# A large tile for the high parts of a pair, and wide blocks for the attention projection

## The chip, the cores and the metric
The kernel runs on one core of a Trainium2 chip. The metric is the time of one execution on the device, in microseconds (us). Before the change it is 1595.82 us, the median of three runs (1594.87 to 1597.53).

## The reference
One decoder layer over 256 tokens of width 2048, all in float32. `u` is the normed input. One projection `u @ w_in` gives q, k, v, z, xBC, dt and two gates. Attention and a state space mixer run side by side, each is projected to the model width, and the two are merged by gates:

```
out_a = attn @ w_attn_br[i]                      # (256 x 1024) @ (1024 x 2048)
out_s = y @ w_ssd_br[i]                          # (256 x 2048) @ (2048 x 2048)
merged = sigmoid(g_a) * out_a + sigmoid(g_s) * out_s
h = h + merged @ w_o[i]
h = h + (silu(f @ w_gate[i]) * (f @ w_up[i])) @ w_down[i]     # hidden width 5632
h = h + sigmoid(rmsnorm(h, g_ple[i]) @ w_ple_gate[i]) * (p[i] @ w_ple_proj[i])
```

## The kernel before
**Three products for one.** Every large product is made of float32 values split in a high part (a cast to the type fp32r) and a low part (value minus high part). A product is high x high, high x low and low x high, three matmuls of 128 x 128 by 128 x 512. The weights are read from memory in raw tiles `wr` of two rows of 128 and 512 columns (512 KB, pool of 4). ScalarE casts one into `wh` (pool of 4), VectorE subtracts into `wl` (pool of 3), and PE multiplies.

**Two kinds of blocks.** `nblock` (L178) makes one block of 512 output columns for both halves of the tokens. Each raw tile feeds 12 matmuls. `wide_block` (L281) makes two column blocks at once and goes over pairs `kp` of rows of 128. A plain pair takes two raw tiles and 24 matmuls. A pair listed in `forms` is done as a 2 x 2 x 2 product in seven block products instead of eight, 21 matmuls. For it VectorE makes four sums of the weights, `tr` (L329), which need both raw tiles; the sums are split into `th` (ScalarE, L337) and `tl` (VectorE, L338). Of the raw tiles, three quarters are also used as they are: both rows of the first one (`b11`, `b21`) and the second row of the second (`b22`), here called the plain blocks of the pair. They too are split on L337 and L338. PE takes first the products with the plain blocks (nine matmuls), then those with the four sums. The other factor of the seven products, the token forms, is prepared earlier (`token_forms`, L268). After the last such pair of a block four of the seven sums are combined into `mid` (L353 to L356), and after the block's end `settle` (L359) or `add_settled` (L364) joins them with the plain sums.

The pair's plain blocks use the pools of all plain tiles: two tiles of `wh` and two of `wl`, of which the second is only half used. `tr`, `th`, `tl`, `mid` and all activations come from the pool `big` of 17 tiles.

**The order of the work.** The attention projection is four `nblock`s over `attnT` (L985 to L989), each followed by two multiplications with the gate. Side work (transposes, the mixer, token forms) is queued in `side` and `heads` and taken from the queues by `pump` after each raw tile. A scheduler orders the program and gives each pool tile its place; an instruction waits for the last reader of the tile that had the place before. Each engine takes its instructions strictly in the order of its own queue.

The stages that matter: four `nblock`s for the first gate (L967), the attention projection (454 to 499 us), then wide blocks only: the second gate, the mixer's projection, `w_o`, eleven hidden blocks of gate and up, and three times two down blocks (to 1465 us). 40 pairs are done in seven products.

Of the kernel before, what the change touches and what calls it, by code (L numbers as in the profile page):

```python
# [15 lines left out]
ALU = mybir.AluOpType  # L16
# [45 lines left out]
def block_kernel(ctx: ExitStack, tc: tile.TileContext, x, x_t, p_t, positions, vecs, rows, g_final,  # L62
# [14 lines left out]
    def big(shape, dtype=F32, name="big"):  # L77
        return big_p.tile(shape, dtype, name=name, tag="big")
# [24 lines left out]
    def drain(*queues):  # L103
        for q in queues or (side,):
            while q:
                q.popleft()()
# [52 lines left out]
    def stat(tiles, k):  # L159
        return tiles[k // 4][:, 0, k % 4, :], tiles[k // 4][:, 1, k % 4, :]  # L160
# [10 lines left out]
    def rsqrt_mean(parts, out_r):  # L171

        n = out_r.shape[1]
        s = stat_p.tile([P, NT], F32, name="rms_s")[:, :n]
        nc.vector.tensor_reduce(out=s, in_=parts, op=ALU.add, axis=AX.X)
        nc.gpsimd.tensor_tensor(out=out_r, in0=s, in1=mhalf[:, :n], op=ALU.pow)
# [83 lines left out]
    def joined(tiles, kp):  # L260

        ks = slice(2 * (kp % 2), 2 * (kp % 2) + 2)
        sc = roll("fsc").rearrange("p (j t) -> p j t", j=2)
        src = tiles[kp // 2].bitcast(F32)
        nc.vector.tensor_tensor(out=sc, in0=src[:, 0, ks], in1=src[:, 1, ks], op=ALU.add)
        return sc
# [14 lines left out]
    def wide_block(halves, lhs, nk, forms, pumps=1):  # L281
# [19 lines left out]
        for kp in range(np_):  # L301
# [23 lines left out]
            for o, x, y in ((tr[:, 0], raw[0][:, 0], raw[1][:, 0]),  # L325
# [2 lines left out]
                            (tr[:, 3], tr[:, 2], raw[0][:, 1])):  # L328
                nc.vector.tensor_tensor(out=o, in0=x, in1=y, op=ALU.add)  # L329
            split = []  # L330
            for x, xh, xl in (
                    (raw[0], whi_p.tile([P, 2, NB], F32R, name="wh", tag="wh"),
                     wlo_p.tile([P, 2, NB], F32R, name="wl", tag="wl")),
                    (raw[1][:, 1:2], whi_p.tile([P, 2, NB], F32R, name="wh", tag="wh")[:, 1:2],
                     wlo_p.tile([P, 2, NB], F32R, name="wl", tag="wl")[:, 1:2]),
                    (tr, big([P, 4, NB], F32R, name="th"), big([P, 4, NB], F32R, name="tl"))):
                nc.scalar.copy(out=xh, in_=x)  # L337
                nc.vector.tensor_tensor(out=xl, in0=x, in1=xh.bitcast(F32), op=ALU.subtract)  # L338
                split.extend((xh[:, i], xl[:, i]) for i in range(x.shape[1]))
# [29 lines left out]
    def form_tiles(pairs, name):  # L369
        tile = big([P, 2, 4, 2, P], F32R, name=name)  # L370
        return {kp: tile[:, i] for i, kp in enumerate(pairs)}

    def column_pair(w, col0, jj):
        return tuple((w, col0 + (2 * jj + q) * NB) for q in range(2))
# [333 lines left out]
    def queue_xs(g, src):  # L708
# [69 lines left out]
        def flip(i):  # L778
            def run():
                xd = mix[g, "xd"]  # L780
                kp = 2 * g + i
                if kp == YPAIRS[0]:
                    yforms.update(form_tiles(YPAIRS, "yforms"))
                transpose_pair([xd[:, t, 1] for t in range(NT)], i * 2 * P, yT[g], 2 * i,
                               [vcol(V_GSSD, 4 * g + 2 * i + j) for j in range(2)],
                               yforms.get(kp))
            return run
# [176 lines left out]
    def cols(j):  # L964
        return slice(j * NB, (j + 1) * NB)

    for j in range(4):  # L967
        accs = nblock(w_in, GAO + j * NB, lhs_u, KD)
        for t in range(NT):
            nc.scalar.activation(out=merged[t][:, cols(j)], in_=accs[0][t], func=AF.Sigmoid,  # L970
                                 scale=r1[:, t:t + 1])
    drain(heads)
    UPAIRS = (3, 6)
    uforms = {}

    def u_forms(kp):
        def run():
            if kp == UPAIRS[0]:
                uforms.update(form_tiles(UPAIRS, "uforms"))
            token_forms(joined(uT, kp), uforms[kp])  # L980
        return run

    side.extend(u_forms(kp) for kp in UPAIRS)
    r2 = const.tile([P, NT], F32, name="r2")
    for j in range(4):  # L985
        accs = nblock(w_attn_br, j * NB, lambda k: stat(attnT, k), 8)
        for t in range(NT):
            nc.vector.tensor_tensor(out=merged[t][:, cols(j)], in0=accs[0][t],
                                    in1=merged[t][:, cols(j)], op=ALU.mult)  # L989

    drain()
    rsqrt_mean(ssq2, r2)
    mergedT = []

    def queue_flip(src, dst, j, gbase=None, forms={}):
# [17 lines left out]
        gates.append(parts)  # L1013
    mforms = form_tiles((5,), "mforms")
    for jj in range(2):
        sums, parts = wide_block(column_pair(w_ssd_br, 0, jj), lambda k: stat(yT, k), KD, yforms)
        for i in range(4):
            t, c = i // 2, cols(2 * jj + i % 2)
            settle(i, sums, parts)
            nc.vector.scalar_tensor_tensor(out=parts[i], in0=parts[i], scalar=r2[:, t:t + 1],  # L1020
                                           in1=gates[jj][i], op0=ALU.mult, op1=ALU.mult)
            nc.vector.tensor_tensor(out=merged[t][:, c], in0=merged[t][:, c], in1=parts[i],
                                    op=ALU.add)
        for q in range(2):
            queue_flip(merged, mergedT, 2 * jj + q, None, mforms)
# [239 lines left out]
```

## Time and profile before

| what | us |
|---|---|
| median of three runs | 1595.82 |
| lowest, highest | 1594.87, 1597.53 |
| the profiled execution | 1594.49 |
| its span, first to last instruction | 1592.8 |
| PE busy | 1574.0 (99%) |
| VectorE (DVE) busy | 1201.3 (75%) |
| ScalarE (ACT) busy | 844.2 (53%) |
| GpSimd (POOL) busy | 132.1 (8%) |

PE is matmul, PEld its weight load. The granted clock of PE is 0.998 of full over the span. Matmuls overlap in their pipeline: one of 512 columns shows some 0.39 us from its start to its end, but the next starts after 0.227 us. So what a product costs, and what PE loses at a wait, is read from start to start. A number in brackets at the end of a row is the engine's idle time before the row and what ended it.

### The profile page before, as it was taken

To read this page: it belongs to the slowest core of one execution; us is meant where nothing else is said; L and a number is where in the kernel's file an instruction comes from. 1 tells how busy PE (TensorE), PEld (TensorE's weight loads), DVE (VectorE), ACT (ScalarE), POOL (GpSimd) and SP (SyncE) were. 2 spreads that over 40 slices of the span, in tenths; PEclk is the share of its full clock that TensorE was granted. 3 is DMA by queue.
4 is the path that set the end of the run, shared out by engine and by line. 5 is a ranking of instruction groups with operands and counts; after the bars stand their busy time and mean duration, and the time that the engine had idled before them with its cause. 6 is when DMAs were issued, how large, how long until landed. Compare 5 with 4: busy or idle time off the path is not lost.

```text
span 1592.8 us, 19985 instructions
## 1 busy us (share of the span) xinstructions
PE 1574.0 (99%) x7298; PEld 1300.5 (82%) x7298; DVE 1201.3 (75%) x1507; ACT 844.2 (53%) x1073; POOL 132.1 (8%) x136
## 2 busy tenths in 40 slices
PE   9999999999999999999999999999999999999997
PEld 7988888888888888788788888788888878888886
DVE  8776766666666768788888788887878788788874
ACT  6654665555644554445655554455545444556653
POOL 1014224143210000000000000000000000000000
PEclk9999999999999999999999999999999999999999
DMA  8666435555646666655566655566665566655672
GB/s 270 177 198 185 136 105 158 158 161 157 178 157 183 210 199 213 209 195 189 173 199 195 198 188 197 185 210 193 193 196 177 194 203 199 220 189 185 200 228 87
DMA packets 152562, 296.63 MB, mean 186 GB/s; under 512 B 9536, under 2 KB 9664, under 8 KB 152080
## 3 DMA queue, kind: packets, MB, share of 16 engines
q1 hardware_dynamic: 151168, 290.76, 58.3%
q0 software_dynamic: 576, 3.47, 0.7%
q8 instruction: 57, 0.93, 0.2%
q10 hardware_dynamic: 720, 1.14, 0.2%
q14 instruction: 41, 0.34, 0.1%
HBM read 293.23 MB, written 2.10 MB: 185 GB/s over the span
## 4 chain that ended last, share of the span: by engine, by line
PE 92%; DVE 2%; DMA 2%; ACT 2%; issue 1%; POOL 0%; POOLq 0%; DVEq 0%; SPq 0%; ACTq 0%
PE aux L249 29%; PE acc L249 27%; PE acc L204 9%; PE acc L206 9%; PE acc L205 9%; PE aux L150 1%; DMA wr<-in_w_in_dram 1%; PE aux L754 1%; DMA wr<-in_w_gate_dram 1%; ACT th L337 1%; PE acc L150 1%; DVE tl L338 1%; PE aux L935 1%; PE aux L693 0%; ACT sc L899 0%
## 5 line engine op out<-in xcount | busy, mean ns | idle before, releaser
L309 ACT CAST wh<-wr 128x1024 fp32r<-128x1024 f32 x280 | 293.6, 1053 | 269.4 <-PE acc L249 97.2
L311 DVE TENSOR_TENSOR wl<-wr,wh 128x1024 fp32r<-128x1024 f32 x280 | 337.3, 1221 | 88.2 <-issue 35.8
L195 DVE TENSOR_TENSOR wl<-wr,wh 128x1024 fp32r<-128x1024 f32 (+1 forms) x172 | 227.6, 1330 | 119.6 <-PE acc L205 87.4
L193 ACT CAST wh<-wr 128x1024 fp32r<-128x1024 f32 (+1 forms) x172 | 173.7, 1013 | 167.9 <-PE acc L206 125.6
L249 PE MATMUL aux<-wh,flipT 128*128 128x512 f32 x736 | 237.8, 392 | 0.0
L249 PE MATMUL acc<-wh,flipT 128*128 128x512 f32 x640 | 208.4, 393 | 0.0
L204 PE MATMUL acc<-wh,uT 128*128 128x512 f32 (+1 forms) x512 | 200.3, 391 | 0.7 <-ACT cb L481 0.7
L206 PE MATMUL acc<-wh,uT 128*128 128x512 f32 (+1 forms) x512 | 194.2, 379 | 0.0
L205 PE MATMUL acc<-wl,uT 128*128 128x512 f32 (+1 forms) x512 | 193.9, 379 | 0.0
L249 PEld LDWEIGHTS aux<-wh,flipT 128*128 128x128 f32 x736 | 138.1, 188 | 28.3
L249 PE MATMUL aux<-wl,flipT 128*128 128x512 f32 x368 | 143.8, 391 | 0.6 <-DVE wl L311 0.6
L337 ACT CAST wh<-wr 128x1024 fp32r<-128x1024 f32 x80 | 66.8, 837 | 140.2 <-PE aux L249 62.4
L249 PEld LDWEIGHTS acc<-wh,flipT 128*128 128x128 f32 x640 | 120.2, 188 | 24.6 <-ACT wh L337 0.2
L249 PE MATMUL acc<-wl,flipT 128*128 128x512 f32 x320 | 124.6, 389 | 0.0
L338 DVE TENSOR_TENSOR tl<-tr,th 128x2048 fp32r<-128x2048 f32 x40 | 91.7, 2292 | 26.2 <-ACT th L337 26.1
L204 PEld LDWEIGHTS acc<-wh,uT 128*128 128x128 f32 x512 | 96.3, 188 | 18.1 <-issue 1.4
L205 PEld LDWEIGHTS acc<-wl,uT 128*128 128x128 f32 x512 | 96.4, 188 | 17.6 <-issue 1.0
L206 PEld LDWEIGHTS acc<-wh,uT 128*128 128x128 f32 x512 | 96.2, 188 | 17.8
L337 ACT CAST th<-tr 128x2048 fp32r<-128x2048 f32 x40 | 76.5, 1911 | 51.7 <-DVE tr L329 51.7
L249 PE MATMUL aux<-wh,actT 128*128 128x512 f32 x292 | 95.3, 393 | 0.0
L249 PE MATMUL acc<-wh,actT 128*128 128x512 f32 x292 | 93.6, 390 | 0.0
L338 DVE TENSOR_TENSOR wl<-wr,wh 128x1024 fp32r<-128x1024 f32 x80 | 76.2, 954 | 7.8 <-PE aux L249 4.0
(476 smaller groups left out, 2741.4 us busy)
## 6 DMA issues: line engine op xcount, KB each, us to landing
wr<-in_w_in_dram SPq DMA_DIRECT2D x144, 512.0 KB, 3.7
wr<-in_w_gate_dram SPq DMA_DIRECT2D x88, 512.0 KB, 3.7
wr<-in_w_up_dram SPq DMA_DIRECT2D x88, 512.0 KB, 4.1
wr<-in_w_down_dram SPq DMA_DIRECT2D x88, 512.0 KB, 4.4
wr<-in_w_ssd_br_dram SPq DMA_DIRECT2D x32, 512.0 KB, 4.3
wr<-in_w_o_dram SPq DMA_DIRECT2D x32, 512.0 KB, 4.0
wr<-in_w_ple_gate_dram SPq DMA_DIRECT2D x32, 512.0 KB, 4.9
wr<-in_w_in_dram SPq DMA_DIRECT2D x32, 256.0 KB, 3.9
```

The source lines that it names most:

```text
L150: nc.tensor.transpose(out=ps[:, j, t * P:(t + 1) * P], in_=src[t][:, c:c + P], identity=ident)
L193: nc.scalar.copy(out=wh, in_=wr)
L195: nc.vector.tensor_tensor(out=wl, in0=wr, in1=wh.bitcast(F32), op=ALU.subtract)
L204: nc.tensor.matmul(o, hi[:, ts], wh[:, kk, cs], start=(k == 0), stop=False)
L205: nc.tensor.matmul(o, hi[:, ts], wl[:, kk, cs], start=False, stop=False)
L206: nc.tensor.matmul(o, lo[:, ts], wh[:, kk, cs], start=False, stop=(k == nk - 1))
L249: nc.tensor.matmul(self.tile, a, b, start=self.first, stop=self.left == 0)
L309: nc.scalar.copy(out=wh, in_=wr)
L311: nc.vector.tensor_tensor(out=wl, in0=wr, in1=wh.bitcast(F32), op=ALU.subtract)
L337: nc.scalar.copy(out=xh, in_=x)
L338: nc.vector.tensor_tensor(out=xl, in0=x, in1=xh.bitcast(F32), op=ALU.subtract)
L754: nc.tensor.matmul(ps[:, es], m[:, t, e, :], xd[:, t, 0, es], start=True, stop=True)
```

## The change
The change has two parts. First, in a pair of seven products the high parts of the plain blocks go to a tile `sh` of the pool `big`, which also holds the low part of `b22`. The pair now takes no tile of `wh`, one of `wl` and four instead of three of `big`. Second, the attention projection becomes two wide blocks, with the pair `APAIR` = 2 of four in seven products. Its token forms lie in the free half of the tile of `yforms`. They and the two forms of `uT` are queued before the first gate's blocks, which pump one time more every fourth raw tile, and both queues are drained before the attention projection.

```diff
             split = []
+
+            sh = big([P, 4, NB], F32R, name="sh")
             for x, xh, xl in (
-                    (raw[0], whi_p.tile([P, 2, NB], F32R, name="wh", tag="wh"),
-                     wlo_p.tile([P, 2, NB], F32R, name="wl", tag="wl")),
-                    (raw[1][:, 1:2], whi_p.tile([P, 2, NB], F32R, name="wh", tag="wh")[:, 1:2],
-                     wlo_p.tile([P, 2, NB], F32R, name="wl", tag="wl")[:, 1:2]),
+                    (raw[0], sh[:, 0:2], wlo_p.tile([P, 2, NB], F32R, name="wl", tag="wl")),
+                    (raw[1][:, 1:2], sh[:, 2:3], sh[:, 3:4]),
                     (tr, big([P, 4, NB], F32R, name="th"), big([P, 4, NB], F32R, name="tl"))):
...
-                    yforms.update(form_tiles(YPAIRS, "yforms"))
+                    yforms.update(form_tiles(YPAIRS + ("free",), "yforms"))
...
+    APAIR = 2
     side.extend(u_forms(kp) for kp in UPAIRS)
+    side.append(lambda: token_forms(joined(attnT, APAIR), yforms["free"]))
+    for j in range(4):
+        accs = nblock(w_in, GAO + j * NB, lhs_u, KD,
+                      before=lambda c: pump(1) if c % 4 == 1 else None)
+        for t in range(NT):
+            nc.scalar.activation(out=merged[t][:, cols(j)], in_=accs[0][t], func=AF.Sigmoid,
+                                 scale=r1[:, t:t + 1])
+    drain(heads, side)
     r2 = const.tile([P, NT], F32, name="r2")
-    for j in range(4):
-        accs = nblock(w_attn_br, j * NB, lambda k: stat(attnT, k), 8)
-        for t in range(NT):
-            nc.vector.tensor_tensor(out=merged[t][:, cols(j)], in0=accs[0][t],
-                                    in1=merged[t][:, cols(j)], op=ALU.mult)
-
-    drain()
     rsqrt_mean(ssq2, r2)
+    for jj in range(2):
+        sums, parts = wide_block(column_pair(w_attn_br, 0, jj), lambda k: stat(attnT, k), 8,
+                                 {APAIR: yforms["free"]})
+        for i in range(4):
+            t, c = i // 2, cols(2 * jj + i % 2)
+            settle(i, sums, parts)
+            nc.vector.tensor_tensor(out=merged[t][:, c], in0=parts[i], in1=merged[t][:, c],
+                                    op=ALU.mult)
```

In numbers of instructions: PE 6 matmuls fewer, VectorE 32 instructions more, ScalarE 4 more; the transfers of weights are the same 512 KB tiles, as many as before.

Three places show how the queues move. The first is ScalarE's queue at the second pair of seven products in the last down block of the second third (around 1270 us in the trace of before): a cast of 128x1024 on L337 is the first raw tile of the pair, one of 128x512 its `b22`, and L309 casts plain tiles. Before:

```order
L309 CAST wh<-wr 128x1024 x4
L337 CAST wh<-wr 128x1024
L337 CAST wh<-wr 128x512
L337 CAST th<-tr 128x2048
L309 CAST wh<-wr 128x1024 x2
```

And now:

```order
L309 CAST wh<-wr 128x1024 x4
L337 CAST sh<-wr 128x1024
L337 CAST sh<-wr 128x512
L309 CAST wh<-wr 128x1024
L337 CAST th<-tr 128x2048
L309 CAST wh<-wr 128x1024 x3
```

A plain cast has moved ahead of the large one, and the plain blocks are cast into `sh`.

The second is VectorE's queue at the same pair; L311 makes plain low parts. Before:

```order
L329 TENSOR_TENSOR tr<-wr 128x512
L311 TENSOR_TENSOR wl<-wr,wh 128x1024
L329 TENSOR_TENSOR tr<-wr 128x512
L329 TENSOR_TENSOR tr<-tr,wr 128x512 x2
L338 TENSOR_TENSOR wl<-wr,wh 128x1024
L338 TENSOR_TENSOR tl<-tr,th 128x2048
L338 TENSOR_TENSOR wl<-wr,wh 128x512
L311 TENSOR_TENSOR wl<-wr,wh 128x1024 x2
```

And now:

```order
L329 TENSOR_TENSOR tr<-wr 128x512 x2
L329 TENSOR_TENSOR tr<-tr,wr 128x512
L338 TENSOR_TENSOR sh<-wr,sh 128x512
L311 TENSOR_TENSOR wl<-wr,wh 128x1024
L329 TENSOR_TENSOR tr<-tr,wr 128x512
L338 TENSOR_TENSOR wl<-wr,sh 128x1024
L338 TENSOR_TENSOR tl<-tr,th 128x2048
L311 TENSOR_TENSOR wl<-wr,wh 128x1024 x3
```

The small low part (128x512) has moved from behind the large `tl` to the middle of the sums.

The third is VectorE's queue in the attention projection. Before, in the second and third of the four blocks:

```order
L195 TENSOR_TENSOR wl<-wr,wh 128x1024 x3
L988 TENSOR_TENSOR merged<-acc,merged 128x512
L195 TENSOR_TENSOR wl<-wr,wh 128x1024
L988 TENSOR_TENSOR merged<-acc,merged 128x512
L195 TENSOR_TENSOR wl<-wr,wh 128x1024 x3
```

Now, from the pair of the first wide block to the second raw tile of the next (`mid` on L356 combines, on L361 settles; the multiplication is L996 of the changed kernel):

```order
L311 TENSOR_TENSOR wl<-wr,wh 128x1024 x3
L338 TENSOR_TENSOR tl<-tr,th 128x2048
L356 TENSOR_TENSOR mid<-mid,acc 128x512 x3
L361 TENSOR_TENSOR mid<-aux,mid 128x512
L356 TENSOR_TENSOR mid<-mid,acc 128x512
L996 TENSOR_TENSOR merged<-mid,merged 128x512
L361 TENSOR_TENSOR mid<-aux,mid 128x512 x2
L996 TENSOR_TENSOR merged<-mid,merged 128x512 x2
L361 TENSOR_TENSOR mid<-aux,mid 128x512
L311 TENSOR_TENSOR wl<-wr,wh 128x1024
```

Between the third plain low part and the next one there are now twelve instructions, where one multiplication stood.

## Rows read from the trace of the kernel before

**Rows 1.** Chain that ended last, in order of time: start us, us, what.
```profile
499.15 16.32 PE aux L249 x72
...
823.67 1.61 PE aux L249 x6
```
**Rows 2.** Stretches: us; PE, PEld, DVE, ACT, POOL busy (count); clock, DMA, GB/s.
```profile
454.00:499.00 45.00, 45.00 (x203) 37.03 (x202) 30.21 (x41) 20.63 (x26) 3.71 (x3) 1.00 0.57 177
499.00:584.00 85.00, 84.85 (x375) 69.97 (x374) 64.80 (x70) 43.73 (x44) 0.00 (x0) 1.00 0.65 199
...
sum 1011.00, PE 1005.55 PEld 824.11 DVE 803.46 ACT 516.74 POOL 7.59; mean PE 125.69 PEld 103.01 DVE 100.43 ACT 64.59 POOL 0.95
```
**Rows 3.** Waits of PE, 499 to 1470: who, for whom, us, times, longest.
```profile
PE acc L249 <- DVE wl L338: 3.6, 3, 1.6
PE acc L249 <- DVE tl L338: 0.7, 1, 0.7
PE aux L249 <- DVE wl L311: 0.6, 1, 0.6
PE aux L249 <- DVE tl L338: 0.2, 1, 0.2
PE aux L249 <- DVE wl L338: 0.2, 1, 0.2
```
**Rows 4.** Time line of PE: start us, us, operation, idle before.
```profile
657.11 0.39 PE L249 MATMUL acc<-wh,yforms 128*128 128x512 f32 x1
659.15 0.50 PE L249 MATMUL acc<-wl,yforms 128*128 128x512 f32 x1 [1.65 <-DVE wl L338]
...
1015.21 0.39 PE L249 MATMUL acc<-wh,aforms 128*128 128x512 f32 x1
1016.25 0.50 PE L249 MATMUL acc<-wl,aforms 128*128 128x512 f32 x1 [0.66 <-DVE wl L338]
...
1275.08 0.39 PE L249 MATMUL acc<-wh,aforms 128*128 128x512 f32 x1
1276.75 0.50 PE L249 MATMUL acc<-wl,aforms 128*128 128x512 f32 x1 [1.28 <-DVE wl L338]
```
**Rows 5.** Time line of VectorE, 1246 to 1302 us.
```profile
1257.87 2.29 DVE L338 TENSOR_TENSOR tl<-tr,th 128x2048 fp32r<-128x2048 f32 x1 [1.38 <-ACT th L337]
1260.08 3.49 DVE L311 TENSOR_TENSOR wl<-wr,wh 128x1024 fp32r<-128x1024 f32 x3
1267.93 0.69 DVE L329 TENSOR_TENSOR tr<-wr 128x512 f32<-128x512 f32 x1 [4.36 <-DMA wr<-in_w_down_dram]
...
1273.80 2.29 DVE L338 TENSOR_TENSOR tl<-tr,th 128x2048 fp32r<-128x2048 f32 x1 [0.84 <-ACT th L337]
1276.01 0.69 DVE L338 TENSOR_TENSOR wl<-wr,wh 128x512 fp32r<-128x512 f32 x1
...
1283.61 0.68 DVE L367 TENSOR_TENSOR h<-acc,h 128x512 f32<-128x512 f32 x1
1284.21 0.68 DVE L365 TENSOR_TENSOR h<-h,mid 128x512 f32<-128x512 f32 x1
```
**Rows 6.** Time line of ScalarE at the same pair.
```profile
1268.48 0.62 ACT L337 CAST wh<-wr 128x512 fp32r<-128x512 f32 x1 [1.32 <-PE acc L249]
1271.85 1.92 ACT L337 CAST th<-tr 128x2048 fp32r<-128x2048 f32 x1 [2.75 <-DVE tr L329]
```
**Rows 7.** Time line of VectorE in the second hidden block.
```profile
816.17 1.41 DVE L329 TENSOR_TENSOR tr<-tr,wr 128x512 f32<-128x512 f32 x2
...
821.28 2.29 DVE L338 TENSOR_TENSOR tl<-tr,th 128x2048 fp32r<-128x2048 f32 x1
```
**Rows 8.** Time line of ScalarE in the second hidden block.
```profile
817.59 1.05 ACT L309 CAST wh<-wr 128x1024 fp32r<-128x1024 f32 x1 [2.06 <-PE acc L249]
818.55 1.91 ACT L337 CAST th<-tr 128x2048 fp32r<-128x2048 f32 x1
```
**Rows 9.** The page's first line.
```profile
span 1592.8 us, 19985 instructions
```

More of the change, by code (lines that the diff above doesn't have):

```diff
@@ L965, in cols @@
         return slice(j * NB, (j + 1) * NB)
-    for j in range(4):
-        accs = nblock(w_in, GAO + j * NB, lhs_u, KD)
-        for t in range(NT):
-            nc.scalar.activation(out=merged[t][:, cols(j)], in_=accs[0][t], func=AF.Sigmoid,
-                                 scale=r1[:, t:t + 1])
-    drain(heads)
     UPAIRS = (3, 6)
@@ L981, in u_forms @@
         return run
+    APAIR = 2
     side.extend(u_forms(kp) for kp in UPAIRS)
-    r2 = const.tile([P, NT], F32, name="r2")
-    for j in range(4):
-        accs = nblock(w_attn_br, j * NB, lambda k: stat(attnT, k), 8)
-        for t in range(NT):
-            nc.vector.tensor_tensor(out=merged[t][:, cols(j)], in0=accs[0][t],
-                                    in1=merged[t][:, cols(j)], op=ALU.mult)
-    drain()
-    rsqrt_mean(ssq2, r2)
+    side.append(lambda: token_forms(joined(attnT, APAIR), yforms["free"]))
[6 more added lines that the diff above has]
+    drain(heads, side)
+    r2 = const.tile([P, NT], F32, name="r2")
+    rsqrt_mean(ssq2, r2)
+    for jj in range(2):
[6 more added lines that the diff above has]
+                                    op=ALU.mult)
     mergedT = []
@@ L1015, in block_kernel @@
     for jj in range(2):
-        sums, parts = wide_block(column_pair(w_ssd_br, 0, jj), lambda k: stat(yT, k), KD, yforms)
+        sums, parts = wide_block(column_pair(w_ssd_br, 0, jj), lambda k: stat(yT, k), KD,
+                                 {kp: yforms[kp] for kp in YPAIRS})
         for i in range(4):
```

## Prediction
> **What bounds the kernel now.** I read the stretches first, then the chain of waits, the waits of PE, and last the time lines of the three engines at PE's longest waits. A 512-column product of a stream starts 16.32 / 72 = 0.227 us after the one before it [rows 1]. From 454 to 1465 us PE is idle for 1011.00 - 1005.55 = 5.45 us in all [rows 2]. So PE is the bound, and only two things can shorten the stage: fewer products, or less of these 5.45 us. From 499 us on PE waits 3.6 us in three places and 0.2 us in a fourth for the `wl` of L338, 0.7 and 0.2 us for `tl`, 0.6 us for a plain `wl` [rows 3]. The L338 waits are the small low part of a pair in seven products (128x512, half of the second raw tile). PE started the product that reads it at 659.15, 1016.25 and 1276.75 us, after 657.11, 1015.21 and 1275.08 us for the one before: 2.04, 1.04 and 1.67 us in place of 0.227, a loss of 1.81 + 0.81 + 1.44 = 4.06 us, with the fourth place 4.3 us [rows 3, 4].
>
> Why it is late is seen at 1276 us. VectorE waits 4.36 us for the pair's weights, whose transfers could start only when the three plain low parts of 1260.08 us, queued behind the large `tl` of 1257.87 us, had freed their raw tiles. It then makes the large `tl` at 1273.80 us and only after it the small `wl`, at 1276.01 us [rows 5]. Its high part had been cast at 1268.48 us, after a wait of 1.32 us for PE to free a slot of `wh` [rows 6]. The small part was thus held 2.2 us by an instruction that PE needs later.
>
> **The change part by part.** *Products.* One of four pairs in seven in place of eight block products, in two wide blocks, takes away 2 x 3 = 6 matmuls: 6 x 0.227 = 1.4 us off the path. The Trainium skill (TensorE: Matmul & The Clock Gate, Back-to-back issue gap) gives some 131 ns for a 512-column product in a stream with weight loads; by that the six would be 0.8 us. Rows 1 show 227 ns, which decides.
>
> *High parts in the large tile.* No instruction is added in the 40 pairs that stand. What moves is the order: on VectorE the small low part now stands ahead of the large `tl`, with a plain `wl` between the sums, and on ScalarE both high parts and a plain cast stand ahead of the cast `th`. That cast waits for the last sum (2.75 us at 1271.85 us [rows 6]), and what stood behind it waited too. At 1276 us the small part, two sums after the weights are there, would be done by about 1267.93 + 4 x 0.6 + 1.2 = 1271.5 us, some 4 us before PE asks for it. I take all 4.3 us. Ends: 0, if the weights are what is late, and 4.3.
> PE's waits for `tl` and the plain `wl`, 1.5 us together [rows 3], are less sure. In the hidden blocks the large low part is just in time: made from 821.28 to 823.57 us, taken at 823.67 us [rows 1, 7]. Before, PE had two plain products between the hi products of the large tile and those with `tl`, 0.45 us; in most of these places it now has none. On the other side the cast `th` of 818.55 us stood behind a plain cast that had waited 2.06 us for a slot of PE's [rows 8]; the pair no longer takes two of the four `wh` slots, so that cast can run as soon as its weights land, and `th`, which had its sums by 817.6 us, about 1 us sooner. I take a gain of 0.6 us of the 1.5; ends: 0 and 1.5.
> The large tile comes from the pool of 17. The waits that order prints show its cost in two places alone: the two attention pairs, where `tl` gets its slot only when PE has read `sh`. Everywhere else the waits on these tiles name the engine that makes the data.
>
> *The attention blocks.* VectorE gets 8 sums, 2 large low parts, 8 combinations and 8 settling sums more. Start to start a 512-column sum takes 0.60 us, a plain low part 3.49 / 3 = 1.16, `tl` 2.2 [rows 5]. Per wide block that makes 6 x 1.16 plain, 1.8 for the pair's two low parts, 2.4 of sums, 2.2, and 12 x 0.6 of combining, settling and multiplying: 20.6 us, beside 93 products x 0.227 = 21.1 us on PE. It fits, without room. Two places show:
> - At each block's end VectorE has settle, settle, two multiplications and settle in its queue ahead of the low part of the next block's second chunk. They wait for the third-last products. 5 x 0.6 + 1.2 = 4.2 us, while PE has 3 + 12 + 1 products, less the 0.3 us until an end is seen: 3.35 us. A wait of 0.85 us, twice. Before, the two multiplications of a block stood with a low part between them and PE lost nothing (45.00 of 45.00 us [rows 2]).
> - `tl` of the first pair starts after PE's ninth product and a plain low part, at about 2.55 us of the pair, is done at 4.8, and PE, with 4 hi products and 8 plain ones ahead of it, asks at 21 x 0.227 = 4.76: 0.2 us. The same for the second. Behind `tl` in the queue are the combinations, which wait for its products anyway.
> Sum 2.1 us. Ends: 0 (from 499 to 584 us, with wide blocks and their ends, PE lost 0.15 us [rows 2]), and at each of the two ends the longest wait of before, 1.8, with 0.9 for each `tl`: 5.4.
> The forms of the extra pair (6 VectorE and 1 ScalarE instruction) and those of `uT`, which stood in the attention stage, now stand beside the last sigmoid block. I cost them at nothing, as VectorE has a third of its time free there (30.21 of 45 us in the stretch they come from [rows 2]); were that cover gone, it is the 1.2 us of one plain low part.
>
> The sum: -1.4 - 4.3 - 0.6 + 2.1 = -4.2 us. The profiled execution took 1594.49 us (span 1592.8 [rows 9], and 1.7 around it); it would be 1590.3. The median of the three runs, 1595.82, is 1.33 us above it, so **1591.6 us**.
>
> **The rivals.**
> *The wait moves on (1594.4 us).* The small part is ready, but the large one, now without plain products ahead of it, is late in the same places, and half of the 4.3 us comes back: -1.4 - 2.15 + 2.1 = -1.4. For it: `tl` at 1276 us starts 2.2 us before the small part and would be next. Against it: after the small part PE has two products and four hi products, 1.4 us, and VectorE no longer does the small part's work in between.
> *VectorE becomes the bound in the attention blocks (1601.3 us).* Its 20.6 us of work must fit into 21.1, in order, with waits in it. In the wide blocks that follow it is busy 64.80 of 85 us, 76% [rows 2]; if its waits take the same share here, a block takes 20.6 / 0.76 = 27.0 us, 5.9 over PE's time, 11.8 for two in place of my 2.1: -1.4 - 4.3 - 0.6 + 11.8 = +5.5. It ends over the bound of 0.2% (3.2 us) when the two blocks cost 9.5 us, that is from waits of 5.2 us a block on VectorE. For it: five settling and multiplying instructions a block wait for the block's last products. Against it: three slots of `wl` let it run 5.4 us ahead in the rest of the block, and the waits of rows 2 are mostly spare time.
> *Better than the sum (1587.3 us).* All of PE's waits go: with the start-to-start losses of the three shown and the rest by rows 3, 4.3 + 1.5 = 5.8; with 0.1 us more at each of some 12 restarts, 7.1; and the ends of the attention blocks are as free as those of 499 to 584 us: -1.4 - 7.1 = -8.5.
> The Trainium skill (VectorE: DVE Perf Modes, The DRAIN you can't avoid) has a flush of about the duration less 266 ns after each VectorE instruction before the next starts. On top of a row's 0.68 us that would make the five at a block's end 2 us longer and the forecast 4 us higher. The rows start 0.60 us apart (1283.61, 1284.21 us [rows 5]), so no chance is given to it.
>
> **How the numbers follow.** Forecast 0.50, with 1589.3 to 1593.8 as its own range; the wait moves on 0.22; VectorE the bound 0.13; better 0.15. A change under 0.2%, 3.2 us, can't be told from none here: below 1592.6 is faster, over 1599.0 slower. About four fifths of the forecast and all of the better case lie below 1592.6: 0.56 with rounding; the rest of the forecast and the moved wait between: 0.31; slower 0.13. The range takes in the better case and goes up to 1597.5, past the moved wait.
>
> **What would show it.** The waits of PE for the small low part (now L338 into `sh`) should be gone; those for `tl` should be 1 us or less in sum. In the attention blocks PE should wait about 0.85 us for a plain `wl`, at the second block's 14th product and at the 14th of the block after it, and VectorE be busy nine tenths. The large pairs' weights should land about 1 us earlier at the second pair of a down block. I am wrong if PE's idle time from 499 us on is not below 2 us, if the attention blocks take over 45 us for their 42.2 us of products, or if PE waits for `tl` in the hidden blocks, where it now has no cover.

## The result and the profile after

The changed kernel takes 1617.86 us (median of 4 runs, 1617.07 to 1618.57); the kernel before took 1596.18 us on the same chip. The ratio is 1.0136, with a 95% interval of 1.0118 to 1.0153: slower by 21.7 us, where 1591.6 us was predicted. The first lines of the page after, against [rows 9] and the table of before:

```profile
span 1615.7 us, 19905 instructions
...
PE 1582.7 (98%) x7292; PEld 1302.0 (81%) x7292; DVE 1218.7 (75%) x1539; ACT 849.8 (53%) x1077; POOL 135.4 (8%) x136
```

PE has six matmuls fewer and is busy 8.7 us longer. The stretches of after, with the columns of [rows 2]:

```profile
454.00:499.00 45.00, 42.46 (x187) 34.49 (x186) 36.03 (x42) 21.00 (x22) 0.00 (x0) 1.00 0.59 192
...
776.00:945.00 169.00, 163.29 (x718) 131.64 (x717) 134.80 (x157) 90.09 (x105) 4.96 (x1) 0.99 0.59 185
...
1290.00:1465.00 175.00, 171.33 (x750) 140.22 (x751) 139.68 (x156) 88.51 (x92) 1.11 (x2) 0.98 0.62 199
sum 1011.00, PE 991.80 PEld 807.92 DVE 794.13 ACT 508.32 POOL 7.22; mean PE 123.97 PEld 100.99 DVE 99.27 ACT 63.54 POOL 0.90
```

From 454 to 1465 us PE is idle 19.20 us, not 5.45. The attention projection has 2.54 of them; most of the rest lies in the hidden and down blocks from 776 us on. PE's waits from 499 to 1470 us, to be held against [rows 3]:

```profile
PE acc L249 <- ACT sh L337: 4.7, 3, 3.2
PE acc L249 <- DVE tl L338: 4.1, 4, 1.8
PE acc L249 <- ACT th L337: 2.2, 2, 1.1
PE aux L249 <- DVE tl L338: 1.9, 3, 0.8
PE acc L249 <- DVE wl L311: 1.7, 3, 0.7
PE acc L249 <- DVE wl L338: 1.5, 2, 0.8
PE aux L249 <- DVE wl L311: 0.3, 2, 0.2
PE aux L249 <- ACT sh L337: 0.2, 1, 0.2
```

The small low part is waited for nowhere any more (the `wl` of L338 is now the large one of `b11` and `b21`). But the pair's high parts `sh` and `th`, which cost PE nothing before, now cost 7.1 us, and `tl` 6.0 in place of 0.9.

One place in slow motion: the first hidden block of the second third. PE, from the block's first product on:

```profile
1035.92 0.39 PE L249 MATMUL aux<-wh,flipT 128*128 128x512 f32 x1
...
1048.16 0.84 PE L249 MATMUL aux<-sh,hforms 128*128 128x512 f32 x3
1050.10 0.49 PE L249 MATMUL acc<-th,hforms 128*128 128x512 f32 x1 [1.10 <-ACT th L337]
1052.43 0.50 PE L249 MATMUL acc<-tl,hforms 128*128 128x512 f32 x1 [1.83 <-DVE tl L338]
```

ScalarE from the end of the block before to there:

```profile
1026.06 1.05 ACT L309 CAST wh<-wr 128x1024 fp32r<-128x1024 f32 x1 [0.60 <-DMA wr<-in_w_down_dram]
1027.60 1.05 ACT L309 CAST wh<-wr 128x1024 fp32r<-128x1024 f32 x1 [0.49 <-DMA wr<-in_w_gate_dram]
1028.91 1.05 ACT L309 CAST wh<-wr 128x1024 fp32r<-128x1024 f32 x1 [0.26 <-DMA wr<-in_w_up_dram]
1029.87 0.58 ACT L353 COPY mid<-aux 128x512 f32<-128x512 f32 x1
...
1042.03 0.63 ACT L337 CAST sh<-wr 128x512 fp32r<-128x512 f32 x1 [3.90 <-DMA wr<-in_w_up_dram]
1044.57 1.06 ACT L309 CAST wh<-wr 128x1024 fp32r<-128x1024 f32 x1 [1.91 <-DMA wr<-in_w_gate_dram]
1047.20 1.06 ACT L309 CAST wh<-wr 128x1024 fp32r<-128x1024 f32 x1 [1.57 <-DMA wr<-in_w_up_dram]
1048.15 1.90 ACT L337 CAST th<-tr 128x2048 fp32r<-128x2048 f32 x1
```

VectorE in the same time:

```profile
1027.69 3.49 DVE L311 TENSOR_TENSOR wl<-wr,wh 128x1024 fp32r<-128x1024 f32 x3
1031.10 0.69 DVE L365 TENSOR_TENSOR h<-h,mid 128x512 f32<-128x512 f32 x1
...
1037.29 1.22 DVE L311 TENSOR_TENSOR wl<-wr,wh 128x1024 fp32r<-128x1024 f32 x1
1038.42 1.29 DVE L367 TENSOR_TENSOR h<-acc,h 128x512 f32<-128x512 f32 x2
1039.62 2.36 DVE L311 TENSOR_TENSOR wl<-wr,wh 128x1024 fp32r<-128x1024 f32 x2
...
1045.17 0.69 DVE L329 TENSOR_TENSOR tr<-tr,wr 128x512 f32<-128x512 f32 x1
...
1050.08 2.29 DVE L338 TENSOR_TENSOR tl<-tr,th 128x2048 fp32r<-128x2048 f32 x1 [2.49 <-ACT th L337]
```

Read it from the end. `tl` follows `th` at once; `th` starts at 1048.15 us, though its last sum is done at 1045.86, because the plain cast ahead of it waits until 1047.20 us for its weights. Those weights were asked for at 1042.01 us, since a raw tile came free only then, by the second plain `wl` of 1039.62 us, which stands behind the additions to `h`. SyncE's queue (the load at 1038.58 us is the pair's own `up` tile):

```profile
1038.58 0.37 SPq L298 DMA_DIRECT2D wr<-in_w_up_dram  x1
...
1042.01 0.37 SPq L298 DMA_DIRECT2D wr<-in_w_up_dram  x1
```

The additions run late because the copy that begins them, `mid` of L353, stands at 1029.87 us behind three plain casts, each of which waited for its weights (0.60, 0.49 and 0.26 us). VectorE for its part starts the first addition (1031.10 us) only when the three low parts made from such casts (1027.69 us on) are done. The last addition ends 3.79 us after the block's first product. In the kernel before, the same product starts at 1025.04 us and the last addition ends 1.75 us after it; its VectorE, ScalarE and SyncE there:

```profile
1025.51 1.28 DVE L367 TENSOR_TENSOR h<-acc,h 128x512 f32<-128x512 f32 x2
...
1034.35 0.69 DVE L329 TENSOR_TENSOR tr<-tr,wr 128x512 f32<-128x512 f32 x1
```

```profile
1035.46 1.91 ACT L337 CAST th<-tr 128x2048 fp32r<-128x2048 f32 x1
```

```profile
1027.96 0.37 SPq L298 DMA_DIRECT2D wr<-in_w_up_dram  x1
...
1030.23 0.37 SPq L298 DMA_DIRECT2D wr<-in_w_up_dram  x1
```

`th` starts 10.42 us after the block's first product there, 12.23 us now. The pair's own data are not later than before: its `up` tile is asked for 2.66 us after the block's first product (2.92 before), and the last sum is done 9.94 us after it (10.00 before). What came later is the load for the plain cast that now stands ahead of `th`: 6.09 us after the block's first product, against 5.19. PE, too, asks for `tl` sooner: if `th` had been in time, 13.15 us after the block's first product against 14.46 before, because other products that stood between `th` and `tl` now come behind. Thus two queue effects, the block's end and the casts ahead of `th`, offer themselves; the experiments try to take them apart. The expectations call this theory Q, or Q2: the freed high tiles let plain casts come ahead of `th` and of the copy, and those casts wait for weights.

Behind its three longest losses PE also ran at half clock for a while. In a stretch around 1320 us (the third column from the end is PEclk, the granted clock):

```profile
1321.00:1326.00 5.00, 5.00 (x14) 3.84 (x13) 2.32 (x4) 1.46 (x2) 0.00 (x0) 0.50 0.64 199
```

From 1328 to 1332 us it is 1.00 again. At half clock a product starts 0.427 us after the one before. 27 such steps in the trace make 27 x 0.200 = 5.4 us of the 21.7.

### The profile page after: what moved, and what is told of

Read it like the earlier page. It is cut to its first block, busy times and chain, and to the rows that moved or that the text cites. A ratio compares the mean times of both kernels' runs of the same rounds, so it can differ in the third digit from the quotient of the medians.

```text
span 1615.7 us, 19905 instructions
## 1 busy us (share of the span) xinstructions
PE 1582.7 (98%) x7292; PEld 1302.0 (81%) x7292; DVE 1218.7 (75%) x1539; ACT 849.8 (53%) x1077; POOL 135.4 (8%) x136
## 4 chain that ended last, share of the span: by engine, by line
PE 85%; DVE 5%; DMA 4%; ACT 3%; issue 1%; POOL 0%; POOLq 0%; DVEq 0%; ACTq 0%; SPq 0%
PE aux L249 28%; PE acc L249 27%; PE acc L204 8%; PE acc L205 8%; PE acc L206 7%; DMA wr<-in_w_up_dram 2%; DVE wl L311 2%; DVE tl L338 1%; ACT th L337 1%; PE aux L150 1%; DVE tr L329 1%; DMA wr<-in_w_in_dram 1%; DMA wr<-in_w_down_dram 1%; DVE wl L195 1%; PE aux L754 1%
## 5 line engine op out<-in xcount | busy, mean ns | idle before, releaser
L309 ACT CAST wh<-wr 128x1024 fp32r<-128x1024 f32 x292 | 307.4, 1054 | 374.5 <-PE aux L249 112.0
L311 DVE TENSOR_TENSOR wl<-wr,wh 128x1024 fp32r<-128x1024 f32 x292 | 351.5, 1221 | 64.6 <-PE aux L249 26.8
L195 DVE TENSOR_TENSOR wl<-wr,wh 128x1024 fp32r<-128x1024 f32 (+1 forms) x156 | 207.2, 1335 | 98.7 <-PE acc L205 74.7
L193 ACT CAST wh<-wr 128x1024 fp32r<-128x1024 f32 (+1 forms) x156 | 156.7, 1008 | 138.6 <-PE acc L206 98.9
L249 PE MATMUL aux<-wh,flipT 128*128 128x512 f32 x688 | 221.3, 393 | 0.0
L249 PE MATMUL acc<-wh,flipT 128*128 128x512 f32 x592 | 189.5, 393 | 0.0
L249 PEld LDWEIGHTS aux<-wh,flipT 128*128 128x128 f32 x688 | 129.9, 189 | 26.9
L249 PEld LDWEIGHTS acc<-wh,flipT 128*128 128x128 f32 x592 | 111.2, 188 | 22.7
L338 DVE TENSOR_TENSOR tl<-tr,th 128x2048 fp32r<-128x2048 f32 x42 | 96.3, 2292 | 27.3 <-ACT th L337 27.3
L205 PEld LDWEIGHTS acc<-wl,uT 128*128 128x128 f32 x512 | 96.3, 188 | 17.8 <-issue 1.0
L329 DVE TENSOR_TENSOR tr<-wr 128x512 f32<-128x512 f32 x84 | 55.4, 688 | 73.1 <-DMA wr<-in_w_up_dram 31.9
L206 PEld LDWEIGHTS acc<-wh,uT 128*128 128x128 f32 x512 | 96.2, 188 | 17.8
L337 ACT CAST sh<-wr 128x1024 fp32r<-128x1024 f32 x84 | 69.2, 836 | 64.2 <-DMA wr<-in_w_up_dram 27.7
L337 ACT CAST th<-tr 128x2048 fp32r<-128x2048 f32 x42 | 80.3, 1911 | 33.6 <-DVE tr L329 33.4
```

What stands on the lines that cost most here:

```text
L193: nc.scalar.copy(out=wh, in_=wr)
L195: nc.vector.tensor_tensor(out=wl, in0=wr, in1=wh.bitcast(F32), op=ALU.subtract)
L205: nc.tensor.matmul(o, hi[:, ts], wl[:, kk, cs], start=False, stop=False)
L206: nc.tensor.matmul(o, lo[:, ts], wh[:, kk, cs], start=False, stop=(k == nk - 1))
L249: nc.tensor.matmul(self.tile, a, b, start=self.first, stop=self.left == 0)
L309: nc.scalar.copy(out=wh, in_=wr)
```

## Experiments

What PE loses is summed below from the trace's PE rows: of every start-to-start step between two products of split weights (512 columns, in `nblock` and `wide_block`) that is clearly longer than 0.227 us (some 0.28 us or more), the part over 0.227 us, by stage (us). The sums are of one profiled execution each. All kernels ran beside the kernel before; the ratio is to it. "High" is the number of high-part tiles (of the pool of 4) that a pair holds.

| kernel | high | median, us | ratio (95%) | to 454 | 454-500 | 500-776 | 776-1490 |
|---|---|---|---|---|---|---|---|
| before | 2 | 1596 | 1 | 7.2 | 0.6 | 3.8 | 11.3 |
| changed | 0 | 1617.86 | 1.0118-1.0153 | 7.5 | 3.1 | 4.9 | 30.5 |
| 1 large tile alone | 0 | 1614.08 | 1.0099-1.0129 | 7.2 | 0.6 | 5.2 | 28.0 |
| 2 attention alone | 2 | 1595.58 | 0.9986-1.0005 | 7.5 | 0.2 | 3.3 | 13.1 |
| 3 low part alone | 2 | 1596.28 | 0.9988-1.0007 | 7.2 | 0.6 | 4.1 | 11.3 |
| 4 high parts alone | 0 | 1619.01 | 1.0128-1.0159 | 7.2 | 0.6 | 5.9 | 33.5 |
| 5 `th` first, large tile | 0 | 1659.66 | 1.0378-1.0414 | 7.2 | 0.6 | 18.1 | 57.6 |
| 6 `th` first, small tiles | 2 | 1595.90 | 0.9992-1.0011 | 7.2 | 0.6 | 2.6 | 12.9 |
| 7 half | 1 | 1589.73 | 0.9936-0.9969 | 7.2 | 0.6 | 3.9 | 7.0 |
| 8 three high tiles | 0 (of 3) | 1605.26 | 1.0036-1.0066 | 10.3 | 0.6 | 6.0 | 14.7 |
| 9 the other half | 1 | 1597.07 | 1.0002-1.0021 | 7.2 | 0.6 | 4.3 | 13.1 |
| 10 copy on VectorE | 0 | 1603.52 | 1.0029-1.0062 | 7.2 | 0.6 | 6.5 | 17.4 |
| 11 half and attention | 1 | 1594.30 | 0.9983-1.0001 | 7.5 | 4.7 | 4.6 | 7.2 |
| 12 half, five raw tiles | 1 (of 3) | 1598.02 | 1.0002-1.0020 | 10.2 | 0.6 | 6.2 | 7.5 |
| 13 gate on `th` | 0 | 1616.85 | 1.0120-1.0147 | 7.2 | 0.6 | 4.4 | 28.2 |
| 14 gate and copy | 0 | 1620.87 | 1.0146-1.0174 | 7.2 | 0.6 | 4.3 | 36.4 |
| 15 half again | 1 | 1591.93 | 0.9965-0.9983 | 7.2 | 0.6 | 4.9 | 7.3 |
| 16 half and copy | 1 | 1594.76 | 0.9987-1.0004 | 7.2 | 0.6 | 4.9 | 10.4 |
| 17 copy, kernel before | 2 | 1598.99 | 1.0006-1.0025 | 7.2 | 0.6 | 2.9 | 15.1 |
| 18 copy, changed kernel | 0 | 1611.61 | 1.0066-1.0109 | 7.5 | 5.8 | 6.0 | 25.3 |

In the changed kernel the four sums have grown from 22.9 to 46.0 us; less 1.4 us for the six products, that is the 21.7 us by which it is slower.

**Which part (1 to 4).** Kernel 1 is the first hunk of the change alone, kernel 2 all the others. Kernels 3 and 4 cut the first hunk in two (the high parts stay in `wh`; or the low parts stay in `wl`):

```diff
 kernel 3
+            sh = big([P, 4, NB], F32R, name="sh")
                     (raw[1][:, 1:2], whi_p.tile([P, 2, NB], F32R, name="wh", tag="wh")[:, 1:2],
-                     wlo_p.tile([P, 2, NB], F32R, name="wl", tag="wl")[:, 1:2]),
+                     sh[:, 3:4]),
 kernel 4
+                    (raw[0], sh[:, 0:2], wlo_p.tile([P, 2, NB], F32R, name="wl", tag="wl")),
+                    (raw[1][:, 1:2], sh[:, 2:3],
+                     wlo_p.tile([P, 2, NB], F32R, name="wl", tag="wl")[:, 1:2]),
```

> The large tile alone, the attention projection as before. Theory Q (queue order): a pair no longer takes two of the 4 buffers for high parts, so plain tiles are cast and split one further ahead and stand in front of the pair's th cast and of the end-of-block chain on ScalarE and VectorE; TensorE runs dry at the first blocks of the hidden layer. Of the 23.2 us by which the stalls beyond a 227 ns step grew, 2.9 lie in the attention blocks, so this kernel should carry the other 20: 1616 us (1612 to 1619). Theory A (the attention projection is to blame, with its shifted side work): 1592 to 1598.

> The attention projection in wide blocks alone, the pair's parts in the small buffers as before. Theory Q: 6 products fewer (-1.4 us) against some 2.9 us of stalls at its pair: 1597.7 us (1595 to 1600), and no half clock after 454 us. Theory A: 1610 or more.

> Only the small low part (the low part of b22) goes to a large tile; both high parts stay in the 4 small buffers; attention as before. Theory Q: the pair still holds two high buffers, so the order around the th cast and the block ends stays as before, and the 3.8 us of waits for the small low part go: 1593 us (1591 to 1597). Rival P (pool pressure: one more tile out of the pool of 17 for each pair makes tr, th, tl and mid wait for a slot): this kernel takes as many large tiles as the large-tile kernel, so it should be as slow: 1610 to 1617.

> Only the two high parts go to a large tile; both low parts stay in the 3 small low buffers; attention as before. Theory Q: the high buffers are what was freed, and the order on ScalarE shows one to two plain casts ahead of th: 1608 to 1618. Rival L (the low buffers freed by the change let VectorE run ahead): within 1594 to 1600. Rival P: 1610 to 1617 as well, so P is told by the kernel with the low part alone.

The large tile is to blame, and of it the high parts. Kernel 3 takes as many tiles of the pool of 17 and is as fast as before, so the pool is not the cause. It is not faster, though: the small low part is waited for nowhere, and the waits have moved on, as its PE waits from 499 us on show:

```profile
PE aux L249 <- DVE wl L311: 1.6, 3, 0.7
PE acc L249 <- DVE wl L311: 1.2, 2, 0.7
PE acc L249 <- DVE tl L339: 1.1, 3, 0.6
PE aux L249 <- DVE tl L339: 0.9, 3, 0.6
PE aux L249 <- ACT wh L309: 0.2, 1, 0.2
```

5.0 us in all, against 5.3 in [rows 3]: plain `wl` and `tl` have taken over.

**How many high tiles a pair holds, and the order of its splits (5 to 8).** Kernels 5 and 6 write the split of `tr` ahead of the two others, in the large-tile kernel and in the kernel before. Kernel 7 leaves `b11` and `b21` in a small tile; kernel 8 takes one small tile away:

```diff
 kernels 5, 6: this entry of the tuple becomes the first
                     (tr, big([P, 4, NB], F32R, name="th"), big([P, 4, NB], F32R, name="tl")),
 kernel 7, against kernel 1
-                    (raw[0], sh[:, 0:2], wlo_p.tile([P, 2, NB], F32R, name="wl", tag="wl")),
+                    (raw[0], whi_p.tile([P, 2, NB], F32R, name="wh", tag="wh"),
+                     wlo_p.tile([P, 2, NB], F32R, name="wl", tag="wl")),
 kernel 8, against kernel 1
-    whi_p = ctx.enter_context(tc.tile_pool(name="whi", bufs=4))
+    whi_p = ctx.enter_context(tc.tile_pool(name="whi", bufs=3))
```

> The large-tile kernel (attention as before), with the pair's three splits written in another order: th and tl first, then the plain blocks' parts. The same tiles, pools and instructions; only their order on the engines moves: th now stands ahead of the pair's own casts and of all later plain casts on ScalarE, and the copy that begins the end-of-block chain has no plain cast more ahead of it than in the kernel before. Theory Q (queue order): the stalls at the first hidden blocks (3.4 us each) and the half clock behind them go, 1598 us (1593 to 1604); what may be late instead are the pair's small low parts, now behind tl's 2.29 us. Rival R (it is the large tile itself, its slot or its sharing by four parts): no gain, 1610 or more.

> The kernel before, with the same re-writing of the order alone (th and tl split first; small buffers as before). Theory Q: th is early already in the kernel before, so nothing to gain there, and the small low part comes later by up to tl's 2.29 us where it was waited for at 659 and 1276 us: 1598 us (1594 to 1604). If instead this gains more than 3 us, the order of the pair's splits matters by itself and the large tile's effect in the sister kernel cannot be read as Q alone.

> Between the two: b11 and b21's high part in a small buffer as before, only b22's high and low part in the large tile, so that a pair holds one of the 4 high buffers (two before, none in the large-tile kernel). Theory Q: on ScalarE one plain cast less stands ahead of th than in the large-tile kernel, but three still ahead of the end-of-block copy, as there: between the two, 1604 us (1598 to 1611). Rival R: as slow as the large-tile kernel, 1611 to 1617.

> The large-tile kernel with 3 buffers for high parts in place of 4. Theory Q: plain tiles can run only 3 ahead, the order on ScalarE shows two plain casts in place of three behind th in half of the blocks, one still ahead of it: some of the loss comes back though there is less memory, 1607 us (1600 to 1613). Rival R, or that plain tiles lack buffers: no gain or a loss, 1613 or more.

Kernel 5 went the other way by 46 us. The same tiles and instructions in another order are thus worth more than the whole change, but the order that the theory asked for is bad: the pair's raw tiles come free only behind `th` and `tl`, and loads start late. SyncE's queue in one hidden block of kernel 5 (the stop of 15 us lies between two loads):

```profile
1156.76 0.37 SPq L298 DMA_DIRECT2D wr<-in_w_up_dram  x1
1171.72 0.37 SPq L298 DMA_DIRECT2D wr<-in_w_gate_dram  x1
```

Kernel 8 is 8.8 us faster than kernel 1 with one small tile less, and that although it loses 3.1 us more ahead of 454 us, where pairs have no part. A free high tile does harm here. How it does is only in part shown. At the place in slow motion above, the copy starts 6.03 us ahead of the block's first product in kernel 1, 9.04 us ahead in kernel 8, and `th` 12.13 and 8.11 us behind it. Yet in both, three plain casts stand between the pair's `th` and the copy, so their number is not what counts: in kernel 1 each of the three waited for its weights (0.24, 0.26 and 0.84 us), in kernel 8 none did. Kernel 7, expected between kernel 3 and kernel 1, beats both and the kernel before. It, too, has three casts there that wait for no weights, with the copy 8.99 us ahead of the first product.

Kernel 4 shows that a late copy is not the whole. Only one plain cast stands ahead of its copy, and its additions end 1.33 us after the block's first product (at 1038.92 us), earlier than in the kernel before. Still `th` starts 12.86 us after that product, behind two plain casts that waited for their weights:

```profile
1038.96 1.29 DVE L367 TENSOR_TENSOR h<-acc,h 128x512 f32<-128x512 f32 x2
```

```profile
1051.78 1.91 ACT L337 CAST th<-tr 128x2048 fp32r<-128x2048 f32 x1
```

**The end of a block (9 to 12).** Kernel 9 puts `b22`'s high part into the small tile instead of `b11`'s and `b21`'s. Kernel 10 is kernel 1 with the copy that begins a block's end on VectorE. Kernel 11 is kernel 7 with the attention part (the other hunks of the change), kernel 12 is kernel 7 with five raw and three high tiles.

```diff
 kernel 9, against kernel 1
-                    (raw[1][:, 1:2], sh[:, 2:3], sh[:, 3:4]),
+                    (raw[1][:, 1:2], whi_p.tile([P, 2, NB], F32R, name="wh", tag="wh")[:, 1:2],
+                     sh[:, 3:4]),
 kernel 12, against kernel 7
-    wraw_p = ctx.enter_context(tc.tile_pool(name="wraw", bufs=4))
-    whi_p = ctx.enter_context(tc.tile_pool(name="whi", bufs=4))
+    wraw_p = ctx.enter_context(tc.tile_pool(name="wraw", bufs=5))
+    whi_p = ctx.enter_context(tc.tile_pool(name="whi", bufs=3))
 kernel 10, against kernel 1
-                nc.scalar.copy(out=parts[0], in_=q1.tile)
+                nc.vector.tensor_copy(out=parts[0], in_=q1.tile)
```

> The other half: b11's and b21's high parts in the large tile with b22's low part, b22's high part in a small buffer, so that a pair again holds one of the 4 high buffers; attention as before. Theory Q2 (what counts is how many high buffers a pair holds, since that sets how many later plain casts ScalarE takes up ahead of the pair's th cast and of the block-end copy, and those casts stand waiting for loads): as good as the half kernel, 1590 us (1586 to 1597). Rival S (what counts is which part lies in the large tile): as the large-tile kernel, 1604 to 1616.

> The large-tile kernel (attention as before) with the copy that begins the end-of-block chain (the first block sum out of PSUM) moved from ScalarE to VectorE, so that it cannot stand behind plain casts that wait for loads. Theory Q2: at the first hidden blocks of the second and third group the end-of-block additions came 2.0 us later than in the kernel before, through that copy; that part of the stalls of 3.3 us there goes, and the half clock behind them: 1606 us (1600 to 1611). Rival T (only the th cast's own delay counts): 1612 to 1616. VectorE gets some 0.6 us more per block, 18 blocks.

> The half kernel (b11's and b21's high parts in a small buffer, b22's two parts in the large tile) with the attention projection in wide blocks. The attention part alone gave 1595.6 against 1596.3 and the half kernel alone 1589.7 against 1596.6: 1589 us if the two add up (1586 to 1592). Rival I (interaction: with the large tile the attention part cost 3.8 us, 1617.9 against 1614.1): 1593.

> The half kernel with 5 buffers for raw weights in place of 4 and 3 for high parts in place of 4 (the same memory); attention as before. Theory Q2: loads start earlier, so casts that stand ahead of others wait less for them, but plain tiles have one high buffer less, which cost some 2.6 us ahead of 499 us where three were tried: 1590 us (1585 to 1597). If the loads were not what the casts wait for, 1595 or more.

Kernel 10 gives back 10.6 us of the 17.8. The move changes VectorE's queue as well: the copy stands there between the second and the third plain low part. Its VectorE and ScalarE at the place shown above (the block's first product starts at 1032.32 us here):

```profile
1024.14 0.68 DVE L352 COPY mid<-aux 128x512 f32<-128x512 f32 x1
...
1033.00 1.29 DVE L366 TENSOR_TENSOR h<-acc,h 128x512 f32<-128x512 f32 x2
```

```profile
1040.09 1.05 ACT L309 CAST wh<-wr 128x1024 fp32r<-128x1024 f32 x1 [2.85 <-DMA wr<-in_w_gate_dram]
1041.05 1.90 ACT L336 CAST th<-tr 128x2048 fp32r<-128x2048 f32 x1
```

The additions end 1.97 us after the block's first product, and `th` starts 8.73 us after it, not 12.13 as in kernel 1, though a plain cast still stands ahead of it. PE waits for neither `th` nor `tl` there. Kernel 9, with one high tile held like kernel 7, is 5 to 7 us slower than it and lies between what the two theories said: the number of tiles held is not all that counts. Kernel 11 does not add up: its attention stage loses 4.7 us, where the attention part alone lost 0.2. Kernel 12 pays ahead of 454 us for the missing high tile, as kernel 8 did, and in the hidden and down blocks loses 7.5 us, about as much as with four raw and four high tiles. A fifth raw tile alone, with four high tiles, was not tried.

**The place of `th` alone, and controls (13 to 18).** In kernels 13 and 14 each plain cast behind a pair of the same block multiplies by a column of ones that is made from `th`, so `th` stands ahead of them; this holds the plain casts back, too. Kernel 14 has the copy on VectorE as well.

```diff
+                        nc.scalar.activation(out=wh, in_=wr, func=AF.Copy, scale=one)
...
+            one = stat_p.tile([P, 1], F32, name="one")
+            nc.scalar.activation(out=one, in_=t1[0].bitcast(F32)[:, 0:1], func=AF.Copy,
+                                 scale=0.0, bias=1.0)
```

> The large-tile kernel (attention as before), with every plain cast that follows a pair in its block made to need that pair's th: it is written as a multiplication by a column of ones, and the column (128x1) is made from th. So th stands directly behind the pair's own casts on ScalarE, as in the kernel before; tiles, pools and the place of the block-end copy stay. Theory Q2: th's own delay (1.9 us at the first hidden blocks of the second and third group) goes, the 2.0 us of the block-end copy stay: 1609 us (1603 to 1612). Rival U (th's place does not matter; the rest is the large tile itself): 1613 to 1616.

> Both at once: th kept ahead of later plain casts by the column of ones, and the block-end copy on VectorE; the high parts still in the large tile. Theory Q2: both terms go, and the large-tile kernel is about as fast as the kernel before: 1598 us (1594 to 1602). Rival U: no better than the copy alone, 1603 or more.

> The half kernel once more (b11's and b21's high parts in a small buffer, b22's high and low part in the large tile; attention as before), to tell whether its gain holds: 1589.5 us (1588 to 1592) if it does; 1594 or more if the first result was chance.

> The half kernel with the block-end copy on VectorE. Its TensorE waits from 499 us on are down to some 2 us, so there is little left to win, and VectorE gets 0.6 us more in each of 18 blocks: 1590 us (1587 to 1593). Theory Q2 leaves the sign open; more than 3 us either way would show that block ends matter there too.

> Control: the kernel before with the block-end copy on VectorE. There the copy stands behind two plain casts, not three, and its block ends were not late, so by theory Q2 nothing is won: 1597 us (1594 to 1601), VectorE having 0.6 us more in each of 18 blocks. If it gains 5 us or more, the gain of the copy has nothing to do with the large tile.

> The changed kernel (both parts) with the block-end copy on VectorE. Theory Q2: the same 10.6 us as with the large tile alone, and the half clock at the first hidden blocks of the second and third group goes: 1607 us (1602 to 1612). If the attention part has its own way of making the block ends late, 1612 or more.

The theory fell in its second term, the place of `th`. With `th` ahead of all later plain casts kernel 13 is no faster than kernel 1, and kernel 14 is 17 us slower than kernel 10. From 499 to 1470 us PE in kernel 13 waits for `th` as long as in kernel 1 (2.4 against 2.3 us) and longer for `tl` (9.4 against 7.1). At the place in slow motion `th` starts 11.84 us after the block's first product, against 12.13 in kernel 1: no plain cast is ahead of it, but its last sum is done later (11.80 us after the first product, 10.26 in kernel 1). In kernel 14 the plain low parts are late, 8.9 us against 1.3 in kernel 10, and `th` is waited for again, which kernel 10 had no wait for; the first of PE's waits:

```profile
PE acc L249 <- DVE wl L314: 4.9, 3, 2.1
PE aux L249 <- DVE wl L314: 4.0, 2, 2.0
PE acc L249 <- ACT th L339: 3.3, 4, 1.8
```

At the place of kernel 10's rows kernel 14's additions end early too (1.90 us after the block's first product), yet three plain low parts still stand behind the additions, and PE waits 2.0 us for the first of them. An early block end is therefore not enough by itself. As the gate moves plain casts and not `th` alone, the place of `th` by itself stays untested. The copy gains nothing where the block's end was not late: it costs 2.8 us in the kernel before (17) and 2.8 in the half kernel (16), where the additions at that place end later with it (3.05 us after the block's first product against 1.44 in kernel 15). In the changed kernel (18) it gives 6.3 us, less than in kernel 1: its attention stage loses 5.8 us, 2.7 more than without it (its profiled execution is the slowest of its four, 1616.14 us).

The gain of kernel 7 held: 0.9965 to 0.9983 in the second study (15), 0.9936 to 0.9969 in the first. It is the one version that is clearly faster than the kernel before, by 3 to 7 us.

## Why the prediction was wrong

- *Six products, -1.4 us.* Not contradicted: the attention part alone measured -0.7 us, with an interval of -2.2 to +0.8.
- *The small low part, -4.3 us.* The wait went, as said; the time did not. Alone (kernel 3) its removal is worth nothing, since plain `wl` and `tl` were next. That is the rival in which the wait moves on, for this term. In the half kernel, where nothing else got worse, PE's waits from 499 us on are down from 5.3 to 1.9 us (3.2 in its second study): the gain was there, and the changed kernel could not have it.
- *The step that failed* is the one on the freed high tiles: "the pair no longer takes two of the four `wh` slots, so that cast can run as soon as its weights land, and `th` [...] about 1 us sooner", costed at a gain of 0.6 us. At the one place from which it was read [rows 8] it came true: `th` starts 4.65 us ahead of PE's first product with it, against 3.60 before, and PE waits for nothing there (rows below). In the first hidden block of the second third `th` came 1.8 us later in the block, behind one plain cast more, and PE lost 3.4 us: the step took one place for all. The freed slots are the cause of the loss: freeing them costs 22.8 us (kernel 4), with the low parts left where they were, and freeing none costs nothing (kernel 3). Giving one high tile less returns 8.8 (kernel 8). How the loss comes about is shown in part: moving the block-end copy returns 10.6 (kernel 10), but kernel 4 is as slow without a late copy at the place shown. The prediction had put a price on the wait for a slot, and none on what that wait held back.
- *The pool of 17 costs nothing outside the attention pairs.* Right (kernel 3).
- *Attention, +2.1 us.* The size was near, the place wrong. With both parts the stage lost 3.1 us against 0.6, not at the block ends, where 0.85 us had been put down twice, but at the two pairs, for `tl` (at 472.69 us, 1.1 us) and `th` (at 493.18 us, 1.7 us). Alone it lost 0.2: the 2.1 were no cost of the attention part either, but of the large tile in it. VectorE is busy 36.03 of 45 us there, 80% and not nine tenths, so the rival in which it becomes the bound fell; the only chance given to a slower kernel, 0.13, had rested on that. The forms at nothing: near enough, PE's loss ahead of 454 us grew by 0.3 us.
- *A cost that no step had:* the half clock, 27 x 0.200 = 5.4 us, in the kernel with the large tile alone 14 x 0.200 = 2.8 us.

The rows for the place of [rows 8]: PE in the kernel before, then ScalarE and PE in the changed kernel:

```profile
822.15 0.84 PE L249 MATMUL aux<-th,hforms 128*128 128x512 f32 x3
```

```profile
825.86 1.91 ACT L337 CAST th<-tr 128x2048 fp32r<-128x2048 f32 x1
```

```profile
830.51 0.39 PE L249 MATMUL aux<-th,hforms 128*128 128x512 f32 x1
```

The prediction's own signs of error came true: PE idle from 499 us on is not below 2 us (19.20 - 2.54 = 16.7), the attention blocks take 45.3 us, and PE waits for `tl` in the hidden blocks, where the products that lay between `th` and `tl` had gone.

Open: the last 7 us of kernel 10, where PE still waits 4.3 us for `sh`, at the first pair of three hidden blocks, and 4.1 us for `tl`; why the plain casts of kernel 1 wait for their weights where those of kernels 7 and 8 do not; by which way kernel 4 loses as much as kernel 1; and why it matters which high part stays in the small tile (kernels 7 and 9). Nor is shown how far what kernel 8 gives back and what kernel 10 does are the same time.

## What to carry to other kernels

A pool that is "too small" may be what holds an in-order engine back from working ahead on the wrong tile; before freeing a slot, list what will now be queued earlier and what stands behind it. A queue's head that waits for a transfer costs what is queued behind it, here the copy that opens a block's end, because the plain low parts that free the raw tiles for the next loads stand behind the additions, and those wait for the copy. A wait read at one place tells of that place: look at the same step in the other blocks before it goes into a sum. Removing the wait that a trace shows is worth only the distance to the next late instruction.

## What the runs showed of the hardware that was not expected

PE's granted clock fell from 1.00 to 0.50 (from 2.4 GHz to 1.2) behind some waits; a product then took 0.427 us in place of 0.227. In the changed kernel it fell three times, each time behind one or two waits next to each other that cost 3.4 us, and was back within 3 to 7 us. The length of the wait alone does not tell whether it falls: in kernel 14 it fell behind a single wait that cost 2.0 us (the product starts at 1265.78 us), while in kernel 1 it stayed at 1.00 behind one that cost 2.3 us (at 779.25 us). In kernel 5 it fell behind losses of 2.8, 3.7 and 3.9 us, among others. In the kernel before it did not fall between 7 and 1587 us.
